# Moving the sums of a feed-forward's seven-product way down from VectorE into accumulating DMAs

## The chip, the cores and the metric

The kernel runs on one core of a Trainium2 chip. Time is device microseconds of one execution; a measurement is the median of several. Engines are named as in the profile: PE is TensorE's matmul, PEld its load of weights, DVE is VectorE, ACT is ScalarE, POOL is GpSimd and SP is SyncE, which here only issues DMAs. A name with a q behind it (SPq, POOLq) is that engine's queue of issued DMAs.

## The reference

One decoder layer in float32 on 1024 tokens of width 1024: a SwiGLU feed-forward, a mixer (stick-breaking attention beside Mamba-2), a cross-attention over 256 memory tokens, and a second feed-forward, each between two RMS norms and with a residual. The change lies in the first feed-forward and in the norms that follow it:

```python
def rmsnorm(x, g):
    x32 = x.astype(jnp.float32)
    y = x32 * lax.rsqrt(jnp.mean(x32 * x32, axis=-1, keepdims=True) + EPS)
    return (y * g.astype(jnp.float32)).astype(x.dtype)

def swiglu(h, w_gu, w_down):
    gu = h @ w_gu
    g, u = jnp.split(gu, 2, axis=-1)
    return (jax.nn.silu(g) * u) @ w_down
...
        f = swiglu(rmsnorm(h, ffn1_pre_g[l]), ffn1_w_gu[l], ffn1_w_down[l])
        h = h + 0.5 * rmsnorm(f, ffn1_post_g[l])
```

The hidden width is 2816, that is 22 blocks of 128.

## The kernel before

Activations lie transposed: 128 features on the partitions, tokens along the free axis, in two halves of 512 tokens (`hh` 0 and 1). Every float32 matmul is made of three with operands split into a high and a low part (`split`, lines 263 and 265: ScalarE copies the high part, VectorE subtracts it for the low one), so a product of one 128 by 128 block costs three matmuls of 512 columns.

The way up (`up_phase`) writes silu(g)·u to HBM, in tiles `act_d[b][hh]` of 128 by 2 by 512; b counts 11 pairs of blocks, and the middle index is the block of the pair. Its last rows in `seven` are VectorE's subtraction at line 818, GpSimd's product at 819 and the store of the second half by GpSimd's queue at 821.

The way down (`down_first`) is one step of Strassen's scheme in Winograd's form: the 2 by 2 split of the work (blocks of a pair, halves of the tokens, halves of the output) takes seven products instead of eight, in the order 1, 5, 2, 6, 3, 7, 4. A product runs over 11 units, one for each pair b; a unit is one activation operand and one weight operand, each split, and 12 matmuls into four PSUM banks. `take` hands the units out and prepares operands five units ahead of PE's program. What runs ahead in fact is bounded by buffers: eight `hl` tiles for split activations, eight places for split weights (`place`), and four raw buffers for what `load` (line 961) brings by SP's queue. Products 5, 6, 3 and 7 take sums of activations: product 5 adds the two blocks of the second half into a buffer `keep[b]` (line 1037), product 6 subtracts a block of the first half from it (1049), product 3 subtracts `keep[b]` from another (1055), and product 7 subtracts two loaded blocks in a raw buffer (1059). All of these go through the helper `add`, so the profile shows them under line 976, by the tiles `xh` (where `keep` lies), `wraw` and `raw`. Weight sums (`wsum`, `wdif`) are made on VectorE in the same way, with a third load for products 1 and 2 (`z`).

After product 2, 6, 3 and so on, the PSUM banks are copied or added into the tiles `F` (`copy`, line 999; `update`, line 1003, again line 976 in the profile). When one half of the tokens is complete, `post` puts its norm into a list of due times on the planner's clock, which adds 0.422 ns for each column of a matmul as PE's program is written: column sums (`rms_cols`, on PE with the column `small`, then lines 332 to 339), row factors (`rms_rows`, lines 347 to 369, with two matmuls), and for each of eight blocks the scaling and residual (lines 428 and 432), a store `h<-F`, the split for the next stage, and `presum`, the squares for the next norm. `sumsq` squares on ScalarE (378, 381) and adds up in two accumulators on VectorE (382); with the eighth block it adds the second accumulator to the first (384). `resid` lists loads of the residual on GpSimd's queue (403). Each engine runs its instructions strictly in the order in which a scheduler at build time put them; that scheduler plays the program through with estimated times, and lets an idle engine take an instruction from far ahead if its buffer is free. `urgent` raises an instruction's priority there.

Of the kernel before, what the change touches and what calls it, by code (L numbers as in the profile page):

```python
# [46 lines left out]
class Kern:  # L47
    def __init__(self, nc, tc, ap):
# [9 lines left out]
        self.kept = {}  # L58

# [314 lines left out]
    def sumsq(self, accs, i, src):  # L374
# [8 lines left out]
        if i == KT - 1:  # L383
            self.kp(nc.vector.tensor_tensor(out=accs[0], in0=accs[0], in1=accs.pop(), op=ALU.add))
# [22 lines left out]
    def post(self, hh, gname, r2, gnext=None, out=None, step=None, spread=True, pins=(23000, 28000), accs=None, tail=None, times=None):  # L407
# [36 lines left out]
        def presum(d):  # L444
            if d == 0:
                accs2.extend(self.new_accs())
            self.sumsq(accs2, d, self.F[hh][d])

        T0 = self.clock
        if step is None:  # L450
# [168 lines left out]
    def up_phase(self, sp, sp2, wgu, gpre, act_d, bank, load, plain, sizes, rw=None, begin=None, between=None):  # L619
# [162 lines left out]
        def seven(f):  # L782
# [34 lines left out]
            with self.urgent():  # L817
                self.emptied = nc.vector.tensor_tensor(out=e, in0=e, in1=b, op=ALU.subtract).ins  # L818
# [19 lines left out]
        def up(f, hh, t, w):  # L838
            ps = self.proj_now(w, hh)
            with self.urgent():  # L840
                nc.vector.tensor_tensor(out=t, in0=t, in1=ps, op=ALU.mult)
# [101 lines left out]
    def seven_tools(self, sp, rw, sums_d=None):  # L943
# [34 lines left out]
        def taker(operands, ahead):  # L978
            order = [(p, b) for p in (1, 5, 2, 6, 3, 7, 4) for b in range(NFF // 2)]
            made, taken = [], [0]  # L980

            def take():
                taken[0] += 1
                while len(made) < min(len(order), taken[0] + ahead):
                    made.append(operands(*order[len(made)]))
# [21 lines left out]
    def down_first(self, sp, rw, wdn, act_d, gpost, gnext):  # L1007
# [13 lines left out]
        def operands(p, b):  # L1021
            a, w = (lambda hh, k: act_d[b][hh][:, k, :]), (lambda k, dh: wdn[b, dh, k])
            tile = place() if p == 1 and b < 2 else self.t(sp, [P, 2, H], F32R, "hl", bufs=8)
            if p == 1:
                x, y = load(a(0, 0), w(0, 0))
                d = wdif[b] = held((self.xp, f"xl{int(b > 3)}", KT + 1))
                nc.sync.dma_start(out=d, in_=w(0, 1))
                o = parts(tile, x), parts(place(), y)
                t = wsum[b] = held(spots[b])
                i = add(t, d, y, ALU.subtract)  # L1030
# [3 lines left out]
            if p == 5:  # L1034
                x, y = load(a(1, 0), a(1, 1))
                k = keep[b] = held((self.xp, f"xh{b // KT}{b % KT}", 1))
                add(k, x, y, ALU.add)
                return parts(tile, k), parts(place(), wsum[b])
            if p == 2:
                x, y = load(a(0, 1), w(1, 0))  # L1040
# [6 lines left out]
            if p == 6:  # L1047
                x, y = load(a(0, 0), w(1, 0))
                add(keep[b], keep[b], x, ALU.subtract)
                o = parts(tile, keep[b]), parts(place(), wsum[b])  # L1050
                add(wsum[b], wsum[b], y, ALU.subtract)
                return o
            if p == 3:
                x, y = load(a(0, 1), w(1, 1))
                add(x, x, keep.pop(b), ALU.subtract)
                return parts(tile, x), parts(place(), y)
            if p == 7:
                x, y = load(a(0, 0), a(1, 0))
                add(x, x, y, ALU.subtract)
# [1363 lines left out]
```

## Time and profile before

| | |
|---|---|
| median of 3 timed runs | 2638.12 us (2637.93 to 2639.47) |
| the profiled execution's own time | 2645.18 us |
| its span, first to last instruction | 2643.4 us |
| mean granted clock of TensorE | 0.992 |
| way down of the first feed-forward (product 1 to the last unit of product 4) | 446.7 to about 673 us of the span |

The profile is of one execution, which took 7.06 us longer than the median of the timed runs; places in it are microseconds from the start of its span. Matmuls overlap: two neighbours start 0.227 us apart at full clock, while one is shown with 0.39 us, so PE's work is best read by counting matmuls in a stretch and looking at the granted clock. An idle engine costs time only where PE waits for it.

### The profile page before, as it was taken

The page shows a single profiled execution, that of the slowest core. Times are in us where ns is not written, and L with a number is a line of the kernel's source. Part 1 is how long each engine was busy: PE and PEld are TensorE (multiplying, and loading weights), DVE is VectorE, ACT ScalarE, POOL GpSimd, SP SyncE. Part 2 cuts the span into 40 slices and gives each one's busy share as a digit, 9 for nine tenths or more (in the row PEclk, how much of TensorE's full clock was granted, in tenths as well). Part 3 has the DMA queues.
Part 4 walks back from the last instruction along what each step waited for, and adds up shares of the span by engine and source line. Part 5 has one row for each costly group of instructions (what it writes and reads, how often), then busy time and mean ns, then how long its engine had stood idle before and what let it go on. Part 6 is the DMA issues. An engine that isn't in the chain of part 4 may idle for free.

```text
span 2643.4 us, 36454 instructions
## 1 busy us (share of the span) xinstructions
PE 2576.9 (97%) x12598; PEld 2135.0 (81%) x12598; DVE 1983.2 (75%) x3085; ACT 1262.9 (48%) x2276; POOL 530.8 (20%) x660
## 2 busy tenths in 40 slices
PE   8999999999999999999999998999999999999998
PEld 6788888887777778888888787887878788888887
DVE  7888787888678774777777777775448989895675
ACT  7544443545367783445554445254445433333432
POOL 1555552001100000000000001122012555542000
PEclk9999999999999999999999999999999999999999
DMA  5688887754721226433434458777667455555976
GB/s 209 238 308 302 304 282 252 255 193 158 259 79 45 71 70 196 115 99 108 109 108 115 146 178 323 252 274 252 218 230 272 167 187 203 195 180 210 347 276 218
DMA packets 225241, 528.87 MB, mean 200 GB/s; under 512 B 28064, under 2 KB 35104, under 8 KB 225056
## 3 DMA queue, kind: packets, MB, share of 16 engines
q1 hardware_dynamic: 190432, 419.56, 48.2%
q0 software_dynamic: 27424, 93.87, 9.8%
q10 hardware_dynamic: 7200, 13.11, 1.3%
q8 instruction: 99, 1.62, 0.3%
q14 instruction: 86, 0.70, 0.1%
HBM read 353.41 MB, written 152.04 MB: 191 GB/s over the span
## 4 chain that ended last, share of the span: by engine, by line
PE 79%; DVE 9%; DMA 6%; ACT 3%; issue 2%; POOL 1%; SPq 0%; DVEq 0%; ACTq 0%; POOLq 0%
PE mm L138 45%; PE dn L138 24%; PE z L138 2%; PE ms L138 2%; PE tr L141 2%; PE y L138 1%; PE ms L141 1%; DMA wraw<-act 1%; DMA raw<-act 1%; DVE hl L265 1%; DVE wlo L265 1%; PE seg L138 1%; DMA blk<-h 1%; DVE whi L265 0%; DMA oraw<-mix 0%
## 5 line engine op out<-in xcount | busy, mean ns | idle before, releaser
L138 PE MATMUL mm<-xh,whi 128*128 128x512 f32 x1288 | 511.5, 406 | 11.1 <-ACT xh L270 7.0
L138 PE MATMUL mm<-xh,wlo 128*128 128x512 f32 x1240 | 478.5, 393 | 3.2 <-DVE wlo L265 2.9
L138 PE MATMUL mm<-xl,whi 128*128 128x512 f32 x1188 | 467.8, 394 | 1.0 <-DVE xl L265 0.7
L138 PEld LDWEIGHTS mm<-xh,whi 128*128 128x128 f32 x1288 | 244.1, 189 | 53.6 <-ACT xh L270 6.9
L138 PEld LDWEIGHTS mm<-xh,wlo 128*128 128x128 f32 x1240 | 234.3, 189 | 55.3 <-DVE wlo L265 3.4
L138 PEld LDWEIGHTS mm<-xl,whi 128*128 128x128 f32 x1188 | 225.6, 190 | 34.1 <-DVE xl L265 1.8
L1823 DVE TENSOR_TENSOR_SCAN nb<-nb,begin 128x128 f32<-128x128 f32 (+7 forms) x128 | 171.7, 1352 | 55.0 <-ACT nb L1819 54.4
L1819 ACT ACTIVATE nb<-z,scale 128x128 f32<-128x128 f32 (+2 forms) x192 | 107.8, 580 | 88.8 <-PE z L138 87.7
L263 ACT CAST whi<-wraw 128x1024 fp32r<-128x1024 f32 (+1 forms) x89 | 81.2, 914 | 69.1 <-PE mm L138 39.1
L1856 POOL MEMSET ath<- 128x128 f32 x64 | 13.1, 205 | 499.0 <-PE mm L138 499.0
L265 DVE TENSOR_TENSOR wlo<-wraw,whi 128x1024 fp32r<-128x1024 f32 x61 | 74.4, 1220 | 38.3 <-ACT whi L263 38.0
L138 PE MATMUL dn<-xh,wlo 128*128 128x512 f32 x296 | 101.0, 389 | 0.0
L737 POOL TENSOR_TENSOR wc<-wraw,raw 128x512 f32<-128x512 f32 x57 | 87.5, 1535 | 66.6 <-DVE whi L265 30.7
L737 POOL TENSOR_TENSOR wc<-raw,wraw 128x512 f32<-128x512 f32 x55 | 85.5, 1555 | 66.5 <-DVE wlo L265 31.4
L819 POOL TENSOR_TENSOR ft<-ft,e 128x512 f32<-128x512 f32 x38 | 62.4, 1642 | 144.2 <-DVE e L818 85.7
L650 ACT ACTIVATE ft<-ft 128x512 f32<-128x512 f32 x88 | 55.4, 631 | 75.0 <-DVE ft L649 70.3
L263 ACT CAST ath<-tr 128x512 fp32r<-128x512 f32 (+1 forms) x107 | 58.2, 545 | 67.5 <-PE tr L141 66.1
L138 PE MATMUL dn<-xh,blk 128*128 128x512 f32 x280 | 90.2, 389 | 0.0
L265 DVE TENSOR_TENSOR atl<-tr,ath 128x512 fp32r<-128x512 f32 (+1 forms) x107 | 67.0, 629 | 29.2 <-ACT ath L263 28.9
L138 PE MATMUL dn<-xh,whi 128*128 128x512 f32 x256 | 88.0, 389 | 0.0
L138 PE MATMUL mm<-ath,v 128*128 128x256 f32 x320 | 86.2, 291 | 0.6 <-DVE sq L1838 0.6
L382 DVE TENSOR_TENSOR acc<-acc,sq 128x512 f32<-128x512 f32 x78 | 52.3, 684 | 42.5 <-ACT sq L381 42.2
(586 smaller groups left out, 6667.9 us busy)
## 6 DMA issues: line engine op xcount, KB each, us to landing
whi<-dwhi SPq DMA_DIRECT2D x57, 512.0 KB, 3.4
wlo<-dwlo SPq DMA_DIRECT2D x57, 512.0 KB, 4.2
wraw<-act SPq DMA_DIRECT2D x102, 256.0 KB, 4.4
raw<-act SPq DMA_DIRECT2D x96, 256.0 KB, 4.3
wraw<-in_w_gu SPq DMA_DIRECT2D x44, 512.0 KB, 4.4
raw<-in_w_gu SPq DMA_DIRECT2D x38, 512.0 KB, 4.8
khi<-whi POOLq DMA_DIRECT2D x30, 512.0 KB, 4.6
klo<-wlo POOLq DMA_DIRECT2D x30, 512.0 KB, 6.7
```

Source lines behind the costliest of these rows:

```text
L138: self._pe(self.nc.tensor.matmul(out, lhsT, rhs, start=start, stop=stop, skip_group_check=self.more), cost)
L141: self._pe(self.nc.tensor.transpose(out, src, self.ident if ident is None else ident), 109.0)
L263: self.kp(self.nc.scalar.copy(hi, src))
L265: (eng or self.nc.vector).tensor_tensor(out=lo, in0=src, in1=hi.bitcast(F32), op=ALU.subtract)
L382: self.kp(nc.vector.tensor_tensor(out=accs[i % 2], in0=accs[i % 2], in1=sq, op=ALU.add))
L650: nc.scalar.activation(t, t, AF.Silu)
L737: nc.gpsimd.tensor_tensor(out=t, in0=a, in1=b, op=op)
L819: nc.gpsimd.tensor_tensor(out=t1, in0=t1, in1=e, op=ALU.mult)
L1819: nc.scalar.activation(nb[:, s0:s1], z[:, 0:n], AF.Sigmoid, scale=sc[:, i : i + 1])
L1823: nc.vector.tensor_tensor_scan(out=nb[:, 0:Wd][:, ::-1], data0=nb[:, 0:Wd][:, ::-1], data1=begin[:, S - Wd : S][:, ::-1], initial=0.0, op0 ...
L1856: nc.gpsimd.memset(x[:, 0, :].bitcast(F32), 0.0)
```

## The change

Sums of activations are no longer made by VectorE. A block is loaded, and the second is added to it by a DMA with `accum_op=ALU.add`, issued on GpSimd's queue. [...] Product 5 loads into `keep[b]` itself and accumulates there; products 6 and 3 accumulate one more block each into `keep[b]`, and load only their weight through a raw buffer; product 7 accumulates in the raw buffer. [...]

The loads get a function of their own, `fetch`, which is called up to three units ahead of `operands`. The third load for product 2 (`z`) stays in `operands`.

In the norms, a flag `apart` makes `sumsq` leave the two accumulators as they are, and `rms_cols`, which already runs over the accumulators of a group, then does its column sums for each. `down_first` sets the flag ahead of the first half's squares and again ahead of the second half's; `post` takes its value over for its own `presum` and clears it, and `presum` sets and clears it around its squares.

```diff
-        if i == KT - 1:
+        if i == KT - 1 and not self.apart:
             self.kp(nc.vector.tensor_tensor(out=accs[0], in0=accs[0], in1=accs.pop(), op=ALU.add))
...
         def presum(d):
             if d == 0:
                 accs2.extend(self.new_accs())
+            self.apart = apart
             self.sumsq(accs2, d, self.F[hh][d])
+            self.apart = False
 
         T0 = self.clock
+        apart, self.apart = self.apart, False
...
-                self.emptied = nc.vector.tensor_tensor(out=e, in0=e, in1=b, op=ALU.subtract).ins
+                x, y = (b, e) if begin else (e, b)
+                self.emptied = nc.vector.tensor_tensor(out=e, in0=x, in1=y, op=ALU.subtract).ins
...
-                nc.vector.tensor_tensor(out=t, in0=t, in1=ps, op=ALU.mult)
+                if begin and hh:
+                    nc.vector.scalar_tensor_tensor(out=t, in0=t, scalar=-1.0, in1=ps, op0=ALU.mult, op1=ALU.mult)
+                else:
+                    nc.vector.tensor_tensor(out=t, in0=t, in1=ps, op=ALU.mult)
...
                 while len(made) < min(len(order), taken[0] + ahead):
+                    if fetch:
+                        while len(got) < min(len(order), len(made) + 3):
+                            got.append(fetch(*order[len(got)]))
+                        made.append(operands(*order[len(made)], got[len(made)]))
+                        continue
                     made.append(operands(*order[len(made)]))
...
+        def plus(x, src):
+            nc.gpsimd.dma_start(out=x, in_=src, accum_op=ALU.add)
+
+        def fetch(p, b):
+            a, w = sources(b)
+            if p == 1:
+                d = wdif[b] = held((self.xp, f"xl{int(b > 3)}", KT + 1))
+                x = load(a(0, 0), w(0, 0))
+                nc.sync.dma_start(out=d, in_=w(0, 1))
+                return x
+            if p == 5:
+                k = keep[b] = held((self.xp, f"xh{b // KT}{b % KT}", 1))
+                nc.sync.dma_start(out=k, in_=a(1, 0))
+                plus(k, a(1, 1))
+                return ()
+            if p == 2:
+                return load(a(0, 1), w(1, 0))
+            if p == 7:
+                x = load(a(0, 0))
+                plus(x[0], a(1, 0))
+                return x
+            if p == 4:
+                return load(a(1, 1))
+            x = load(w(1, int(p == 3)))
+            plus(keep[b], a(0, int(p == 3)))
+            return x
...
             if p == 5:
-                x, y = load(a(1, 0), a(1, 1))
-                k = keep[b] = held((self.xp, f"xh{b // KT}{b % KT}", 1))
-                add(k, x, y, ALU.add)
-                return parts(tile, k), parts(place(), wsum[b])
+                return parts(tile, keep[b]), parts(place(), wsum[b])
...
             if p == 6:
-                x, y = load(a(0, 0), w(1, 0))
-                add(keep[b], keep[b], x, ALU.subtract)
                 o = parts(tile, keep[b]), parts(place(), wsum[b])
-                add(wsum[b], wsum[b], y, ALU.subtract)
+                add(wsum[b], wsum[b], got[0], ALU.subtract)
                 return o
             if p == 3:
-                x, y = load(a(0, 1), w(1, 1))
-                add(x, x, keep.pop(b), ALU.subtract)
-                return parts(tile, x), parts(place(), y)
-            if p == 7:
-                x, y = load(a(0, 0), a(1, 0))
-                add(x, x, y, ALU.subtract)
-                return parts(tile, x), parts(place(), wdif.pop(b))
-            (x,) = load(a(1, 1))
-            return parts(tile, x), parts(place(), wsum.pop(b))
-
-        take = taker(operands, 5)
+                return parts(tile, keep.pop(b)), parts(place(), got[0])
+            return parts(tile, got[0]), parts(place(), (wdif if p == 7 else wsum).pop(b))
+
+        take = taker(operands, 5, fetch)
...
         accs = [self.new_accs(), None]
+        self.apart = True
...
         for i in four:
-            update(F[1][0][i], F[1][0][i], ps[i])
+            update(F[1][0][i], F[1][0][i], ps[i], ALU.subtract)
         for i in four:
-            add(F[1][1][i], F[1][1][i], F[1][0][i], ALU.add)
+            add(F[1][1][i], F[1][0][i], F[1][1][i], ALU.subtract)
...
         units = [take() for _ in range(4)]
+        self.apart = True
         accs[1] = [held((rw, tag, 1)) for tag in ("bh", "bl")]
         squares(1, 1, 0)
         for i in four:
             blocks(ps, units, i, False, True)
-            update(F[1][0][i], F[1][0][i], ps[i], ALU.subtract)
+            update(F[1][0][i], F[1][0][i], ps[i])
             self.sumsq(accs[1], 4 + i, F[1][0][i])
```

More of the change, by code (lines that the diff above doesn't have):

```diff
@@ L446, in presum @@
                 accs2.extend(self.new_accs())
+            self.apart = apart
             self.sumsq(accs2, d, self.F[hh][d])
+            self.apart = False
         T0 = self.clock
+        apart, self.apart = self.apart, False
         if step is None:
@@ L976, in add, with taker @@
             return nc.vector.tensor_tensor(out=o, in0=x, in1=y, op=op)
-        def taker(operands, ahead):
+        def taker(operands, ahead, fetch=None):
             order = [(p, b) for p in (1, 5, 2, 6, 3, 7, 4) for b in range(NFF // 2)]
-            made, taken = [], [0]
+            made, taken, got = [], [0], []
             def take():
@@ L1019, in held, with sources, operands @@
             return self.t(pool, [P, H], F32, tag, bufs=bufs)
-        def operands(p, b):
-            a, w = (lambda hh, k: act_d[b][hh][:, k, :]), (lambda k, dh: wdn[b, dh, k])
+        def sources(b):
+            return (lambda hh, k: act_d[b][hh][:, k, :]), (lambda k, dh: wdn[b, dh, k])
+        def plus(x, src):
[23 more added lines that the diff above has]
+            return x
+        def operands(p, b, got):
+            a, w = sources(b)
             tile = place() if p == 1 and b < 2 else self.t(sp, [P, 2, H], F32R, "hl", bufs=8)
             if p == 1:
-                x, y = load(a(0, 0), w(0, 0))
-                d = wdif[b] = held((self.xp, f"xl{int(b > 3)}", KT + 1))
-                nc.sync.dma_start(out=d, in_=w(0, 1))
+                x, y = got
                 o = parts(tile, x), parts(place(), y)
                 t = wsum[b] = held(spots[b])
-                i = add(t, d, y, ALU.subtract)
+                i = add(t, wdif[b], y, ALU.subtract)
                 if b > 1:
@@ L1034, in operands @@
             if p == 5:
-                x, y = load(a(1, 0), a(1, 1))
-                k = keep[b] = held((self.xp, f"xh{b // KT}{b % KT}", 1))
-                add(k, x, y, ALU.add)
-                return parts(tile, k), parts(place(), wsum[b])
+                return parts(tile, keep[b]), parts(place(), wsum[b])
             if p == 2:
-                x, y = load(a(0, 1), w(1, 0))
+                x, y = got
                 z = self.t(*((self.tp, [P, H], F32, "dg", 1) if b % 2 else (self.fp, [P, H], F32, "rpost", 1)))
```

## The prediction

> **What bounds the kernel now.** I read first the page's busy shares, then the busy time by stretches through the way down (447 to 677 us), and then the timeline wherever a stretch was not full. A stretch's row gives the busy microseconds (and instructions) of PE, PEld, DVE, ACT and POOL behind its length, then the granted clock, the DMA share and GB/s.
>
> ```profile
> span 2643.4 us, 36454 instructions
> ...
> PE 2576.9 (97%) x12598; PEld 2135.0 (81%) x12598; DVE 1983.2 (75%) x3085; ACT 1262.9 (48%) x2276; POOL 530.8 (20%) x660
> ...
> 609.37:614.07 4.70, 0.00 (x1) 0.00 (x0) 4.70 (x9) 3.71 (x7) 0.00 (x0) 0.93 0.17 58
> 614.07:615.94 1.87, 1.87 (x9) 1.87 (x9) 1.87 (x4) 0.00 (x0) 0.00 (x0) 0.50 0.51 149
> 615.94:623.41 7.47, 6.47 (x18) 4.57 (x18) 6.97 (x17) 6.46 (x11) 0.00 (x0) 0.71 0.45 140
> 668.31:677.35 9.04, 8.47 (x27) 6.76 (x27) 6.33 (x14) 2.24 (x4) 1.79 (x4) 0.64 0.88 302
> ```
>
> TensorE sets the time: an edit counts only where it fills a hole on PE. In the changed stage there are two, each followed by a granted clock of 0.50 to 0.71. The timeline (start, duration, engine, line; in brackets the idle time before, and its releaser) shows how the first comes about.
>
> ```profile
> 585.86 1.49 DVE L976 TENSOR_TENSOR wraw<-wraw 128x512 f32<-128x512 f32 x2
> ...
> 593.80 2.88 PE L138 MATMUL dn<-hl,whi 128*128 128x512 f32 x12
> 596.52 2.20 PE L138 MATMUL mm<-hl,wlo 128*128 128x512 f32 x9
> ...
> 601.24 0.69 DVE L976 TENSOR_TENSOR raw<-raw 128x512 f32<-128x512 f32 x1 [2.85 <-DMA raw<-act]
> 606.12 0.69 DVE L976 TENSOR_TENSOR wraw<-wraw 128x512 f32<-128x512 f32 x1 [1.18 <-DMA wraw<-act]
> 606.73 0.68 DVE L265 TENSOR_TENSOR hl<-raw,hl 128x512 fp32r<-128x512 f32 x1
> 607.33 2.47 DVE L976 TENSOR_TENSOR F<-F,dn 128x512 f32<-128x512 f32 x4
> 611.53 1.28 DVE L382 TENSOR_TENSOR acc<-acc,sq 128x512 f32<-128x512 f32 x2
> 613.34 0.68 DVE L384 TENSOR_TENSOR acc<-acc,acc 128x512 f32<-128x512 f32 x1
> 614.07 1.87 PE L138 MATMUL dn<-small,acc 128*128 128x1 f32 x8 [4.70 <-DVE acc L384]
> 618.76 1.28 DVE L265 TENSOR_TENSOR hl<-raw,hl 128x512 fp32r<-128x512 f32 x2
> 620.56 0.15 DVE L332 TENSOR_TENSOR cpost<-dn,cpre 128x4 f32<-128x4 f32 x1
> 622.71 0.50 PE L138 MATMUL dn<-dg,onesr 128*128 128x512 f32 x1 [0.91 <-DVE dg L358]
> ```
>
> A unit of 12 matmuls takes 2.72 us (593.80 to 596.52: 0.227 a matmul); product 3 ends and product 7 begins at 596.5. From then the four updates of F could run, but VectorE does them at 607.3: its queue is in order, and ahead of them stand the adds of product 7 (line 1059), each waiting for two loads. The squares follow late, PE stands 4.70 us at the norm's column sums, and its clock halves. In 609.37 to 623.41, 14.04 us, PE does 18 matmuls (4.08 us at full clock) and 8 records of column sums.
>
> **The change part by part.** The 44 adds of products 5, 6, 3 and 7 leave VectorE.
>
> ```profile
> L976 DVE TENSOR_TENSOR raw<-raw 128x512 f32<-128x512 f32 x5 | 3.4, 687 | 4.6 <-DMA raw<-act 4.6
> L263 ACT CAST hl<-raw 128x512 fp32r<-128x512 f32 x14 | 8.6, 618 | 16.6 <-DVE raw L976 14.1 <-PE ms L138 2.2 <-PE dn L138 0.3
> ...
> wraw<-act SPq DMA_DIRECT2D x48, 256.0 KB, 3.9
> ...
> xl<-in_xT POOLq DMA_DIRECT2D x16, 256.0 KB, 5.7
> h<-F POOLq DMA_DIRECT2D x8, 256.0 KB, 3.0
> ...
> 450.88 2.66 POOL L403 DMA_DIRECT2D xl<-in_xT  x5
> 588.90 0.54 POOL L403 DMA_DIRECT2D xl<-in_xT  x1 [135.36 <-DVE wlo L265]
> ```
>
> (A DMA's row ends with the microseconds from issue to landing.) That is 44 by 0.69, 30 us of VectorE, worth nothing by itself. Their second operands go from SP's queue to POOL's as accumulating DMAs: the bytes fetched stay, POOL gains 44 issues of 0.54 us, 24 us, hidden in a queue that waited 135 us here. Each accumulate waits on POOL for the load whose result it adds to; what can stand behind it are residual loads (line 403) and POOL's last product (line 819), needed tens of microseconds later.
>
> No accumulating DMA is in this trace. Its landing is bounded by the nearest rows on POOL's queue: 3.0 us below (the store), and above twice the load, 11.4, if the destination is read and written again at full price. I take 5.7, the load from HBM into SBUF that it is nearest to. In products 5, 6 and 3 the buffer `keep` is free a whole product (29.9 us) earlier, so even 11.4 is hidden. In product 7 it is not: load, accumulate and split share four raw buffers. One turn of a buffer is T = 3.9 + 5.7 + 1.8 (issue 0.54, splits 0.62 on ScalarE and 0.68 on VectorE) = 11.4 us, with ends 8.7 and 17.1. Four buffers, so a unit in 2.85 us against PE's 2.72, and the operands run up to eight units ahead (buffers of `hl`): no hunger on PE.
>
> The clock of the stall, with estimates from these rows. Product 3 begins at 566.6. Its unit 9 can be split when its unit 1 has freed an `hl`, at 572.0, done at 573.2; its raw buffer then serves units 2, 6 and 10 of product 7, split at 573.2 + T, + 2T and + 3T. The F updates stand behind the split of unit 6 (as at 606.73 before): 596.0, so right at PE's 596.5. From the updates to the last square sum took 5.5 us (607.33 to 612.81): done near 602.5, with 6.9 us in hand before PE's 609.37. The stall goes, and would still go at T up to 15. The next thing late is line 332, which stands behind unit 10's split: 607.4 by the sum. PE comes to the row product 16 matmuls after the column sums, at 614.6, and 332 needs 2.15 us up to it (620.56 to 622.71); so it must start by 612.5, which holds to T = 13.1. With five further splits in the same queue I charge 1 us here (ends 0 and, at T = 17.1, 11.9).
>
> The two parts of the sums: line 384 goes, and PE gets twice the column sums.
>
> ```profile
> 679.62 0.95 PE L138 MATMUL ms<-small,bh 128*128 128x1 f32 x8
> 680.44 0.48 PE L138 MATMUL mm<-xl,whi 128*128 128x512 f32 x1
> ...
> 665.84 0.68 DVE L382 TENSOR_TENSOR acc<-acc,sq 128x512 f32<-128x512 f32 x1
> 667.57 0.68 DVE L384 TENSOR_TENSOR acc<-acc,acc 128x512 f32<-128x512 f32 x1
> 668.31 1.87 PE L138 MATMUL ms<-small,acc 128*128 128x1 f32 x8 [2.54 <-DVE acc L384]
> ```
>
> Eight records take 0.82 us warm (679.62 to 680.44), 1.87 cold. At the first norm nothing waits any more, so this is pure cost: 16 records, 1.64 us. First hole after: 4.08 + 1.64 = 5.72 for 14.04, a gain of 8.3, less the 1 us: 7.3. At the next norm (668) PE waited for line 384; the last part ends at 666.52, 1.7 us before 384 did, so the gain is 1.7 less 0.8 (cold: less 1.9), that is 0.9, with ends of a loss of 0.2 and a gain of 5.7 if the whole hole closed (2.54 + 9.04 us, against 4.3 for its 19 matmuls and 1.64 for the records). By the planner's clock the second half stays in one part: `apart` is one flag, set again after seven units of product 4 (46.7 us from the call of `post(0)`), and the last `presum` of the first half, due at 17.5 + 7 x 4.7 + 0.8 = 51.2, clears it before unit and square number 7 (57). So only two of four norms change.
>
> The signs: three products become the three-operand form.
>
> ```profile
> L841 DVE TENSOR_TENSOR ft<-ft,mm 128x512 f32<-128x512 f32 x3 | 2.1, 684 | 0.6 <-PE mm L138 0.6
> L428 DVE SCALAR_TENSOR_TENSOR F<-F,params,rpost 128x512 f32<-128x512 f32 x16 | 11.9, 743 | 2.1 <-ACT rpost L369 2.1
> ```
>
> 3 by 0.06 us, hidden behind PE; uncovered 0.2. The swapped subtractions keep form and count.
>
> Sum: 7.3 + 0.9 = 8.2 us. Against the profiled execution's own 2645.18 that is 2637.0. The timed median is 2638.12, 7.1 us under that execution; carried over whole it gives 2629.9. If those 7.1 us are partly this stall, the gain is smaller.
>
> The Trainium skill (DMA: Bandwidth & Descriptors, Anatomy of one DMA) puts a DMA from GpSimd at about 2.0 us and its bytes over 436 GB/s, an estimate of 2.6 us for 256 KB. The trace has 5.7 for that load, so the trace decides; by the page T were 7.0, the 1 us would not be charged and the sum 9.2.
>
> **The rivals.**
>
> *The wait goes on to the row product.* For it: VectorE's order, with line 332 behind five more splits. At T between 13.1 and 15.8 (where 332 comes at 620.6, as before) the gain falls from 8.2 to nothing; in the middle 4: time 2634. *The accumulate is slow* (T = 17.1): 332 comes 3.9 us later than now, with 0.8 for the records: 5 us more, 2643.
>
> *Product 1 starves: the other side.* `keep` needs no raw buffer, so nothing but their queues holds product 5's 22 transfers back, and idle queues run ahead: five residual loads asked for in product 3 went out at 450.88.
>
> ```profile
> 446.69 2.66 PE L138 MATMUL dn<-whi,wlo 128*128 128x512 f32 x11
> ...
> 452.38 0.33 SPq L961 DMA_DIRECT2D raw<-act  x1
> ...
> 458.09 0.69 DVE L265 TENSOR_TENSOR hl<-raw,hl 128x512 fp32r<-128x512 f32 x1 [2.72 <-ACT hl L263]
> ...
> 440.00:450.00 10.00, 10.00 (x46) 8.29 (x45) 7.03 (x11) 4.18 (x7) 1.61 (x1) 1.00 0.32 105
> 450.00:460.00 10.00, 10.00 (x45) 8.02 (x44) 6.61 (x11) 2.76 (x5) 3.24 (x6) 1.00 0.81 264
> 460.00:470.00 10.00, 10.00 (x45) 8.28 (x45) 9.13 (x16) 7.21 (x14) 0.00 (x0) 1.00 0.95 325
> ```
>
> Unit 6 of product 1, asked for at 452.38, is split at 458.8 and due at 463.0: 4.2 us in hand, with the DMA full. Units 6 to 10 are 15 transfers, 13 us at 300 GB/s. Shared evenly they take 26, and unit 10 (due 473.9) is ready at 479.7: 6 us lost, net 2 gained, 2636. Wholly behind the 22 (5.8 MB, 19 us) unit 6 is 15 us late: net 7 lost, 2645. It decides from 4.2 us of delay, and costs more than the gain from 12.4. Against it: 440 to 450 runs at 105 GB/s, room for 2 MB. The Trainium skill (the same page, Issuing engines are not separate DMA queues) says all queues share the same 16 engines: by that POOL's queue brings no room.
>
> *It does nothing:* the hole is smaller without the profiler, and the doubled records eat the rest: 2637.
>
> **How the numbers follow.** Forecast (2624 to 2633, by T and the second hole) 0.46; wait at the rows 0.17 (half of it beyond 0.2%); slow accumulate 0.10; product 1 starving 0.19 (a third of it slower); nothing 0.08. 0.2% is 5.3 us, about what a measurement of this kernel can tell: faster below 2632.8, slower above 2643.4. Faster 0.46 + 0.08 = 0.54; slower 0.05 + 0.06 = 0.11; for the operation that no row shows I move 0.04 more to slower, one hundredth of it from faster: 0.53, same 0.32, slower 0.15. Predicted 2629.9, range 2624 to 2643.
>
> **What would show it.** Right: no L976 on `raw<-raw`; F updates near 597; column sums at 609 without idle, 16 records; clock 1.0 at 610 to 620; 16 records at the second norm but 8 on `bh`. Wrong: PE idle between 447 and 477; accumulates landing in over 9 us; line 332 after 613.

## The result, and the profile after

The changed kernel takes 2653.53 us (2651.77 to 2656.07), beside 2638.8 us for the kernel before on the same chip: a ratio of 1.0054, 95% interval 1.0042 to 1.0066. By the ratio it is slower by some 14 us, where 8 us less was forecast and 2643 was the top of the range.

The page says that TensorE did the same work in a longer span (2652.4 us for 2643.4): 16 matmul records more, 46 instructions fewer on VectorE, 44 more on GpSimd.

```profile
PE 2580.9 (97%) x12614; PEld 2138.4 (81%) x12614; DVE 1955.5 (74%) x3039; ACT 1261.8 (48%) x2276; POOL 569.0 (21%) x704
```

The busy time by stretches of the changed kernel shows the place: product 1, where PE had been full (10.00 of 10.00 in both stretches before). The columns are as in the prediction.

```profile
450.00:460.00 10.00, 7.64 (x34) 6.01 (x32) 2.37 (x4) 1.36 (x3) 6.77 (x8) 1.00 1.09 314
460.00:470.00 10.00, 2.85 (x7) 2.23 (x8) 2.87 (x5) 3.52 (x7) 1.25 (x2) 0.62 0.86 185
```

The timeline of the changed kernel tells how it comes about (start, duration, engine, line, operation; in brackets the idle time before and what ended it).

```profile
441.15 2.69 POOL L1038 DMA_DIRECT2D xh<-act  x3 [1.17 <-PE dn L139]
441.20 6.41 SPq L1049 DMA_DIRECT2D xh<-act  x7
446.60 5.60 PE L139 MATMUL dn<-whi,wlo 128*128 128x512 f32 x24
...
451.74 0.87 POOL L1038 DMA_DIRECT2D xh<-act  x1 [7.89 <-DMA xh<-act]
...
456.29 1.76 POOL L824 TENSOR_TENSOR ft<-ft,e 128x512 f32<-128x512 f32 x1
...
458.36 1.13 POOL L826 DMA_DIRECT2D act<-ft  x1
...
466.48 0.62 ACT L264 CAST dx<-wraw 128x512 fp32r<-128x512 f32 x1 [15.11 <-DMA act<-ft]
467.15 8.29 PE L139 MATMUL dn<-hl,dx 128*128 128x512 f32 x24 [9.51 <-ACT dx L264]
```

Read from the end: TensorE waits 9.51 us for the first tile of the tag `dx`. ScalarE, in order, has stood 15.11 us in front of that cast, waiting for the store of the last up-projection block, `act<-ft`: the new tile lies in memory that this store still reads. The store went out at 458.36. It and the product ahead of it (line 824) stand on GpSimd behind accumulates of product 5, each of which waits there for its first load to land; from 443.8 to 451.74 GpSimd does nothing but that. SP's next load for product 1 goes out only at 467.85, the one before it at 454.49. Before, the same chain was there, with nothing ahead of it on GpSimd. The timeline of the kernel before, in rows that the prediction did not use:

```profile
448.39 1.61 POOL L819 TENSOR_TENSOR ft<-ft,e 128x512 f32<-128x512 f32 x1 [16.56 <-issue]
450.30 0.58 POOL L821 DMA_DIRECT2D act<-ft  x1 [0.30 <-POOL ft L819]
...
452.73 0.62 ACT L263 CAST dx<-wraw 128x512 fp32r<-128x512 f32 x1 [3.01 <-DMA act<-ft]
```

The cast waited for that store already, 3.01 us, without costing PE anything. The store is 8.1 us later now (458.36 for 450.30), the cast 13.8 us, and product 7 begins at 608.56 for 596.52: 12.0 us lost. The rest of the cast's delay is the landing of the store itself. The DMA issues from 440 to 480 us show it (a row ends with the microseconds from issue to landing), before:

```profile
act<-ft POOLq DMA_DIRECT2D x1, 256.0 KB, 2.4
```

and in the changed kernel:

```profile
act<-ft POOLq DMA_DIRECT2D x1, 256.0 KB, 8.0
```

So product 5's transfers delay the cast twice: 8.1 us by their accumulates' place in GpSimd's queue, and 5.6 us by a slower landing while the DMA engines are full (share 1.09 in 450 to 460, for 0.81 before).

Downstream, some of the loss comes back. The timeline of the changed kernel at the first norm:

```profile
598.59 0.68 DVE L266 TENSOR_TENSOR hl<-raw,hl 128x512 fp32r<-128x512 f32 x1
...
608.56 2.20 PE L139 MATMUL mm<-hl,wlo 128*128 128x512 f32 x9
...
611.70 0.69 DVE L266 TENSOR_TENSOR hl<-raw,hl 128x512 fp32r<-128x512 f32 x1 [0.66 <-ACT hl L264]
612.31 2.47 DVE L984 TENSOR_TENSOR F<-F,dn 128x512 f32<-128x512 f32 x4
...
621.26 1.84 PE L139 MATMUL dn<-small,acc 128*128 128x1 f32 x16
...
627.13 0.15 DVE L333 TENSOR_TENSOR cpost<-dn,cpre 128x4 f32<-128x4 f32 x1
629.49 0.72 PE L139 MATMUL dn<-dg,onesr 128*128 128x512 f32 x1 [2.63 <-DVE dg L359]
...
688.63 0.95 PE L139 MATMUL ms<-small,bh 128*128 128x1 f32 x8
```

The updates of F start 3.8 us after product 7 (10.8 before), so the column sums come without a wait. The row product waits 2.63 us instead.

For all that follows I use two measures. The ratio is timed. The **way down** is read from a trace: from product 1's first matmul to the first column sum on `bh` (446.60 to 688.63, 242.0 us; before 446.69 to 679.62, 232.9). It leaves out what differs from run to run ahead of it.

### The profile page after: what moved, and what is told of

The parts are those of the page before. It is cut to its first block, busy times and chain, and to the rows that moved or that the text cites. A ratio compares the mean times of both kernels' runs of the same rounds, so it can differ in the third digit from the quotient of the medians.

```text
span 2652.4 us, 36498 instructions
## 1 busy us (share of the span) xinstructions
PE 2580.9 (97%) x12614; PEld 2138.4 (81%) x12614; DVE 1955.5 (74%) x3039; ACT 1261.8 (48%) x2276; POOL 569.0 (21%) x704
## 3 DMA queue, kind: packets, MB, share of 16 engines
q0 software_dynamic: 33760, 105.40, 12.3%
## 4 chain that ended last, share of the span: by engine, by line
PE 85%; DVE 6%; DMA 4%; ACT 2%; issue 2%; POOL 0%; SPq 0%; DVEq 0%; ACTq 0%; POOLq 0%
PE mm L139 47%; PE dn L139 27%; PE ms L139 2%; PE z L139 2%; PE tr L142 2%; PE y L139 1%; PE ms L142 1%; PE seg L139 1%; DMA raw<-act 1%; PE st L139 0%; DVE wlo L266 0%; DMA oraw<-mix 0%; ACT whi L264 0%; DVE F L984 0%; DVE xl L273 0%
## 5 line engine op out<-in xcount | busy, mean ns | idle before, releaser
L1887 POOL MEMSET ath<- 128x128 f32 x64 | 13.1, 205 | 499.0 <-PE mm L139 478.8
```

The costliest lines, as they stand in the source:

```text
L1887: nc.gpsimd.memset(x[:, 0, :].bitcast(F32), 0.0)
```

## The experiments

**How far a trace repeats.** The kernel before, unchanged.

> The kernel before once more, for a second profile beside timed runs. In the first comparison the changed kernel is 14.7 us slower by the timed medians (2653.5 against 2638.8), but only 9.2 us by the two profiled executions (2654.4 against 2645.2): the profiled execution of before was 7 us above its timed median, that of after was not. Theory A: the hole at 609 to 623 us (PE idle 4.7 us at the first norm's column sums, then a halved clock) hangs on the DMAs' luck and is small in most executions. Then this profile, at about 2638 us, shows the idle time before the column sums under 2 us and a clock near 1.0 at 610 to 620. Theory B: profiling itself costs the 7 us; then the profile is again near 2645 us with the 4.7 us in it, while the timed runs stay at 2638.

Measured: ratio 1.0004 (0.9994 to 1.0014). Its second profiled execution, timeline:

```profile
614.60 1.67 PE L138 MATMUL dn<-small,acc 128*128 128x1 f32 x8 [2.19 <-DVE acc L384]
...
680.01 0.95 PE L138 MATMUL ms<-small,bh 128*128 128x1 f32 x8
```

The hole that the prediction set out to fill is 2.19 us here, not 4.70; product 1 began at 449.73, so the way down took 230.3 us. Traces of one kernel differ by 2 to 3 us in this measure, and the hole of the first was on the large side. This execution took 2645.18 us, as long as the first profiled one with twice the hole, so neither theory on record fits: the hole alone is not what puts these two above the median.

**The queue on GpSimd, from two sides.** First, every accumulate is ordered behind the last store:

```diff
-            nc.gpsimd.dma_start(out=act_d[f // 2][1][:, f % 2, :], in_=t1)
+            self.stored = nc.gpsimd.dma_start(out=act_d[f // 2][1][:, f % 2, :], in_=t1).ins
...
-            nc.gpsimd.dma_start(out=x, in_=src, accum_op=ALU.add)
+            i = nc.gpsimd.dma_start(out=x, in_=src, accum_op=ALU.add)
+            self._after(i.ins, self.stored)
```

> The changed kernel, with every accumulating DMA ordered behind the last product and the last store of the way up on GpSimd's queue. In the changed kernel's trace PE waits 9.5 us in product 1 for ScalarE's copy into the first dx tile, which waits for that store: the tile lies where the stored buffer lay. Eight accumulates, each waiting for its load, stand ahead of it on GpSimd's queue. Theory A (the queue's order): with the store first the wait is gone, product 7 begins near 597 us instead of 608.6, and the time falls by 10 to 12 us to about 2642. Theory B (the 22 transfers of product 5 fill the DMA engines and product 1's loads come late): the store leaves early but product 1 still waits for its operands, at least 5 us of PE idle between 447 and 477, and the time stays above 2647.

Second, the last block's product goes to VectorE and its store to ScalarE's queue:

```diff
-            nc.gpsimd.tensor_tensor(out=t1, in0=t1, in1=e, op=ALU.mult)
+            last = begin and f == NFF - 1
+            (nc.vector if last else nc.gpsimd).tensor_tensor(out=t1, in0=t1, in1=e, op=ALU.mult)
...
-            nc.gpsimd.dma_start(out=act_d[f // 2][1][:, f % 2, :], in_=t1)
+            (nc.scalar if last else nc.gpsimd).dma_start(out=act_d[f // 2][1][:, f % 2, :], in_=t1)
```

> The changed kernel, with the last block's product made by VectorE and its second half stored by ScalarE's queue: the accumulates keep their places at the head of GpSimd's queue, but nothing that dx waits for stands behind them. Theory A (the queue's order): as good as ordering the store first, about 2642 us, no wait of dx over 4 us. Theory B (DMA engines full): the transfers start as early as in the changed kernel, so PE still idles 5 us or more in product 1, time above 2647.

Measured: 2646.2 us, 1.0027 (1.0016 to 1.0038), and 2642.17 us, 1.0014 (1.0004 to 1.0023), beside 1.0054 for the change. The waits of TensorE from 446 to 640 us, first kernel (waited for: us in total, times, longest):

```profile
PE dn L139 <- DVE dg L359: 2.2, 1, 2.2
PE dn L139 <- ACT whi L264: 1.5, 2, 0.7
PE dn L139 <- ACT wlo L264: 0.6, 1, 0.6
```

And of the second:

```profile
PE dn L139 <- DVE dg L359: 2.4, 1, 2.4
PE dn L139 <- ACT dx L264: 1.3, 1, 1.3
PE dn L139 <- ACT wlo L264: 0.7, 1, 0.7
```

The wait of 9.5 us is gone in both, and 7 to 11 us of the 14 with it (ratio differences of 0.0027 and 0.0040 at 2640 us). What stays in product 1, 2.1 and 2.0 us of waits, is for splits (ScalarE's casts). In the second kernel, 1.3 us of it is the cast into `dx` once more. Its timeline:

```profile
458.38 0.62 ACT L264 CAST dx<-wraw 128x512 fp32r<-128x512 f32 x1 [6.40 <-DMA act<-ft]
```

The last block's two stores go out at 449.46 and 449.83, and the cast still starts 5.65 us later than the 452.73 of before. The stores land in 6.2 and 8.5 us (2.4 and 2.0 before), and the cast waits for the later one: that is the slow landing alone. An estimate from these rows: the cast can come 4.3 us later at no cost (5.65 less 1.3), so the queue's 8.1 us alone would cost 3.8 us and the slow landing costs 1.3; only the two together make the 9.5. The row product's wait stays too.

**Product 5 without accumulates.** Two loads into raw buffers and one add, as before; the rest as changed.

```diff
-                nc.sync.dma_start(out=k, in_=a(1, 0))
-                plus(k, a(1, 1))
-                return ()
+                return load(a(1, 0), a(1, 1))
...
+                add(k, *got, ALU.add)
```

> Product 5 gets its sums by VectorE adds again (two loads into raw buffers, one add); products 6, 3 and 7 keep their accumulating DMAs, the signs and the norm's two parts stay as changed. The queue theory (the 12 us lost in product 1 come from product 5's early transfers: about 9 from accumulates standing ahead of the last store on GpSimd, about 3 from full DMA engines): the last store is ahead of every accumulate and product 5's loads are held back by the raw buffers, so TensorE waits less than 0.7 us in all of product 1, product 7 starts by 597.5 (596.52 in the profile of before, 608.56 in that of the change), column sums near 610 without a wait, the row product still waits 2 to 3 us; timed 2633 to 2638, ratio 0.9975 to 0.9995. The rival that accumulating DMAs are dear wherever they stand (landing slow, VectorE's splits late in products 6, 3, 7): time stays above 2642 and the waits show in products 6, 3 or 7.

Measured: 2640.32 us, 1.0000 (0.9991 to 1.0009). TensorE's waits from 446 to 640 us, complete:

```profile
PE dn L139 <- DVE dg L359: 3.0, 1, 3.0
```

Product 1 is free of waits, as expected; the time is not as low as expected, since the row product still costs 3 us. Product 5's accumulates cost 0.0054, as much as the whole loss of the change.

**Product 7 without accumulates too, so that only products 6 and 3 have them.**

```diff
             if p == 7:
-                x = load(a(0, 0))
-                plus(x[0], a(1, 0))
-                return x
+                return load(a(0, 0), a(1, 0))
...
+            if p == 7:
+                add(got[0], *got, ALU.add)
```

> Only products 6 and 3 keep accumulating DMAs; products 5 and 7 get their sums by VectorE adds again; signs and the norm's two parts stay as changed. By the queue theory product 1 is free of waits as in the kernel with product 5 alone by adds, and the updates of F stand behind product 7's adds on VectorE again: column sums wait 2 to 4 us (2.2 and 4.7 in the two profiles of before), then the two parts cost 0.8 us: timed 2638 to 2642, ratio 0.9995 to 1.001, some 3 us more than with product 7's accumulates. The rival that product 7's slow accumulates make the row product late (line 333 behind unit 10's split): the row product's wait of 2 to 3 us goes here, and the time is the same or lower than with them, 2635 to 2638.

> The kernel with accumulating DMAs in products 6 and 3 alone, a second time, since its first time (2634.58 us, ratio 0.997) came below what was expected. If the gain is real (the hole from 609 to 623 closed, 615.41 at the row product instead of 623.23): 2632 to 2637, ratio 0.9965 to 0.9985. If it was chance: 2638 to 2642.

Measured: 2634.58 us, 0.9970 (0.9958 to 0.9982), and the second time 2634.91 us, 0.9978 (0.9966 to 0.9990): faster than before, against my expectation that the stall at the column sums would return. The timeline of the first of the two:

```profile
572.82 2.00 SPq L969 DMA_DIRECT2D wraw<-act  x4
...
597.17 0.68 DVE L984 TENSOR_TENSOR wraw<-wraw 128x512 f32<-128x512 f32 x1
597.77 0.69 DVE L266 TENSOR_TENSOR hl<-raw,hl 128x512 fp32r<-128x512 f32 x1
598.37 2.48 DVE L984 TENSOR_TENSOR F<-F,dn 128x512 f32<-128x512 f32 x4
...
609.98 1.84 PE L139 MATMUL dn<-small,acc 128*128 128x1 f32 x16
...
611.86 0.16 DVE L333 TENSOR_TENSOR cpost<-dn,cpre 128x4 f32<-128x4 f32 x1 [0.78 <-PE dn L139]
...
615.41 0.39 PE L139 MATMUL dn<-dg,onesr 128*128 128x512 f32 x1
```

Product 7's adds (line 984) are back ahead of the updates of F, and the updates are early all the same. Its loads go out at 572.82, 126.6 us after product 1's start; before it was 580.45, 133.8 us. So it was not product 7's own adds that made the updates late but how late its loads could begin, and they begin earlier when products 6 and 3 bring only their weights through the raw buffers. Line 333 waits for TensorE now, not TensorE for it. The way down took 225.9 and 223.5 us.

The mirror image is product 7 alone with accumulates: product 5 by adds as above, and products 6 and 3 by

```diff
-            x = load(w(1, int(p == 3)))
-            plus(keep[b], a(0, int(p == 3)))
-            return x
+            return load(w(1, int(p == 3)), a(0, int(p == 3)))
...
+            if p in (6, 3):
+                add(keep[b], keep[b], got[1], ALU.add)
```

The second kernel here is the change with only product 7 put back to adds.

> Only product 7 keeps its accumulating DMAs; products 5, 6 and 3 get their sums by VectorE adds (33 adds of 0.69 us more than in the change); signs and the norm's two parts stay. By the queue theory this is as good as the kernel with product 5 alone by adds, since the adds of 5, 6 and 3 lie behind TensorE's work: no wait over 0.7 us in product 1, updates of F near 597 to 600, column sums near 610, timed 2633 to 2638. If VectorE's extra adds matter they delay the updates of F behind product 7's early operands, and the column sums wait 1 to 3 us: 2637 to 2640.

> The change with product 7 alone put back to VectorE adds; products 5, 6 and 3 keep their accumulating DMAs. Theory: product 5's transfers cost product 1 about 12 us whatever product 7 does, and product 7's accumulating DMAs cost about 3 us at the row product by themselves. So product 1 waits 9 to 10 us for dx as in the change, product 7 starts near 608.5, the row product waits less than 1 us: 2648 to 2652, 2 to 5 us under the change. If the accumulates of product 7 were also what slowed product 1: below 2645.

Measured: 2646.31 us, 1.0023 (1.0013 to 1.0034), against expectation, and 2646.68 us, 1.0020 (1.0009 to 1.0031). The timeline of the kernel with product 7's alone:

```profile
621.98 0.80 PE L139 MATMUL dn<-dg,onesr 128*128 128x512 f32 x1 [6.63 <-DVE dg L359]
```

In the kernel with products 5, 6 and 3 TensorE waits only once from 446 to 640 us: 9.5 us for `dx`.

The two costs are apart: product 7's accumulates make the row product wait (6.63 us alone, 2.2 to 3.0 with those of 6 and 3), product 5's make product 1 wait. Product 7's cost 6 to 9 us as timed (1.0000 against 0.9970 and 0.9978; 1.0054 against 1.0020).

**Which of products 6 and 3.** Product 3's accumulates alone, none at all (with the loads still asked for three units ahead, the other new thing in these kernels), and product 6's alone; all three with the sums of squares in one part. The edit is the last one, for product 6, for both, and for product 3. As in the change, all three store the second half's activations negative, so that sums of activations are additions.

> Accumulating DMAs in product 3 alone; products 5, 6 and 7 by VectorE adds; sums of squares in one part; second half negative. If the gain comes from the raw buffers that product 3's activations no longer take just ahead of product 7: as good as with products 6 and 3, updates of F near 599, no wait at the column sums, 168 to 169 us from product 1's start to the row product, 2634 to 2637. If product 6's accumulates are needed too: updates of F between 600 and 606, part of the wait back, 2637 to 2640.

> No accumulating DMA at all: all sums by VectorE adds, with the loads asked for three units ahead as in the change; sums of squares in one part, second half negative. If the gain of products 6 and 3 comes from their accumulating DMAs: product 7's first loads go out 132 to 134 us after product 1's start as before (133.8; 126 to 127 with the accumulates), updates of F 158 to 161 us after it, the column sums wait 2 to 5 us; timed 2639 to 2642. If the earlier loads alone bring it: 2634 to 2637.

> Accumulating DMAs in product 6 alone; products 5, 3 and 7 by VectorE adds; sums of squares in one part. If product 6's accumulates carry the gain: product 7's loads about 127 us after product 1's start, updates of F near 152, 2634 to 2637. If it takes both, so that each alone moves product 7's loads by 2 to 4 us only: updates of F between 154 and 158, part of the wait at the column sums stays, 2637 to 2640.

Measured: 0.9997 (0.9986 to 1.0009), 0.9994 (0.9986 to 1.0003) and 1.0007 (0.9996 to 1.0018): none differs from before. Product 7's first loads go out at 578.82, 578.72 and 579.58, 131.5 to 132.1 us after product 1's start (133.8 and 132.2 in the two traces of before), and the updates of F come 156.9 to 158.4 us after it (160.6 and 158.1 before, 152.1 and 150.8 with both). So neither product alone, nor the earlier loads alone, moves these dates by much more than two traces of one kernel differ; both products together move the loads by 5.6 to 8.5 us. That raw buffers are what is freed fits this, but the runs show only the dates, not the buffer that decides.

**The two parts of the sums of squares.** Alone on the kernel before; taken away from the change; and taken away from the kernel with products 6 and 3. For the first, the change's lines on the flag were put into the kernel before; for the others it is never set:

```diff
-        self.apart = True
+        self.apart = False
```

> The kernel before with nothing changed but the norm's sums of squares left in two parts (the closing add left out, twice the column sums). Column sums: the wait is 0.7 us shorter, 8 more records cost 0.8 us; second norm: 1.7 us less of wait against 0.8. Timed within 1.5 us of before, ratio 0.9994 to 1.0006. The rival that the two parts are what makes the change slow: 2642 or more.

> The changed kernel, with the flag for two parts never set, so that all sums of squares are joined on VectorE as before. Theory A (each doubled set of column sums costs PE 0.8 us, and the second norm's earlier start gives 1.7 back): within 2 us of the changed kernel's 2653.5. Theory B (the doubled sums make up a good part of the loss): 3 us or more below it.

> Accumulating DMAs in products 6 and 3 alone, and the norm's sums of squares closed to one part as in the kernel before. Against the same kernel with two parts: 0.8 us less at the first column sums (8 records instead of 16), 0.9 us more at the second norm by the prediction's own sum: equal within 1 us, 2633 to 2637. The rival that the two parts are needed to close the hole (the column sums wait for the closing add): 2 us or more slower, with the wait at the column sums.

Measured: 2642.36 us, 1.0004 (0.9995 to 1.0013); 2648.59 us, 1.0032 (1.0018 to 1.0046); 2635.09 us, 0.9976 (0.9964 to 0.9987). TensorE's waits of the first, on either side of the two norms:

```profile
PE dn L139 <- DVE dg L359: 2.2, 1, 2.2
...
PE ms L139 <- DVE acc L383: 0.7, 1, 0.7
...
PE dn L139 <- DVE acc L383: 0.2, 1, 0.2
```

At the second norm the wait for the column sums is 0.7 us for 2.54, as the sum had it. Part of what is gained goes on to the row products: the first norm's waits 2.2 us (0.9 and 0.6 before), the second norm's 0.3 us here and 1.5 us in the first kernel with products 6 and 3 (none before). In time the two parts make no difference, alone or in the fastest kernel. In the change itself the timed difference is 5.8 us (1.0054 to 1.0032; the two intervals overlap a little), of which the trace has 1.8 in the way down (240.2 for 242.0); the 9.2 us in product 1 and 3.25 at the row product stay. Where the rest lies I don't know.

**What is left of product 5's cost.** With the last store off GpSimd and product 7 by adds, so that only product 5's transfers are in question (both edits as above):

> The last block's product and store off GpSimd (as in the second kernel of the first set, 2642.17 us), and product 7 by VectorE adds; products 5, 6 and 3 keep their accumulating DMAs. Theory: 2 to 3 us of waits stay in product 1 from product 5's transfers (full DMA engines), nothing at the column sums, and the row product's wait of 2.4 us goes: 2637 to 2640, so 2 to 4 us above the kernel with accumulates in 6 and 3 alone. If full DMA engines do not matter: level with that kernel, 2633 to 2636.

Measured: 2637.33 us, 0.9987 (0.9977 to 0.9998). TensorE's waits from 446 to 640 us:

```profile
PE dn L139 <- ACT dx L264: 1.1, 1, 1.1
PE dn L139 <- ACT whi L264: 0.7, 1, 0.7
```

It beats the kernel before, and the row product's wait is gone. The 1.1 us for `dx` are again the landing of the last block's stores, 8.0 us for the later one. 2.4 us stay above the kernel with products 6 and 3 (0.9987 to 0.9978), which the two intervals do not separate. Then the first loads of product 5 were put later on SP's queue, by an order behind the last load of the third kind in product 1 (lines 1045 and 1049 of the change):

```diff
-                nc.sync.dma_start(out=d, in_=w(0, 1))
+                self.loaded = nc.sync.dma_start(out=d, in_=w(0, 1)).ins
...
-                nc.sync.dma_start(out=k, in_=a(1, 0))
+                self._after(nc.sync.dma_start(out=k, in_=a(1, 0)).ins, self.loaded)
```

> The kernel with the last block's product and store off GpSimd and product 7 by VectorE adds, and besides product 5's first loads ordered behind product 1's last load on SP's queue (the accumulates follow their loads). If product 5's transfers take the DMA engines from product 1's: TensorE's waits for splits in product 1 (1.1 and 0.7 us there) go, product 1's start to the row product takes 168 to 169.5 us instead of 171.5, timed 2634 to 2636. If it is something else: 171 us and 2637 to 2638 as there. The delay might also make product 5's own operands late: then waits in 477 to 507.

Measured: 2640.34 us, 1.0000 (0.9991 to 1.0009). The edit did the reverse of what I meant. Timeline of its SP queue:

```profile
442.18 7.45 SPq L1050 DMA_DIRECT2D xh<-act  x11
```

All 11 went out in one block ahead of product 1's next load at 452.52 (7 did so in the kernel without the order). The wait for `dx` grew from 1.1 to 2.7 us: more early transfers, more delay. Ordered behind product 1's own activation and weight loads, six units further on:

```diff
-                nc.sync.dma_start(out=k, in_=a(1, 0))
+                self._after(nc.sync.dma_start(out=k, in_=a(1, 0)).ins, ones[min(b + 6, 10)])
```

(`ones` keeps the last such load of each unit of product 1.)

> The last block's product and store off GpSimd, product 7 by VectorE adds, and each of product 5's first loads ordered on SP's queue behind product 1's activation and weight loads of six units further on (the last ones behind unit 10's). If product 5's early transfers take the DMA engines from product 1: no wait of TensorE for splits in product 1, units 6 to 10 asked for by about 461 as in the kernel with accumulates in 6 and 3 alone (468 to 477 with the early transfers), product 1's start to the row product 168 to 169.5 us, timed 2634 to 2636. If not: 171 to 172 us, 2637 to 2638. Product 5's own first operands may come late (load, accumulate and split are about 14 us, from 461): then a wait of up to 3 us appears at 476 instead.

Measured: 2638.16 us, 1.0000 (0.9991 to 1.0009). Timeline:

```profile
458.42 6.52 SPq L1051 DMA_DIRECT2D xh<-act  x11
...
499.96 0.69 DVE L985 TENSOR_TENSOR xh<-rpost,xh 128x512 f32<-128x512 f32 x1 [2.85 <-DMA rpost<-in_w_dn]
...
508.74 3.20 PE L139 MATMUL dn<-hl,whi 128*128 128x512 f32 x11 [1.85 <-DVE hl L266]
```

Its DMA queues from 440 to 510 us (q0 is GpSimd's, with the accumulates alone in it; q1 is SP's; packets, MB, and the share of the 16 engines' time), and its DMA issues (median us to landing at the end):

```profile
q0 software_dynamic: 3168, 5.77, 45.2%
q1 hardware_dynamic: 5616, 10.23, 43.4%
...
xh<-act POOLq DMA_DIRECT2D x22, 256.0 KB, 12.9
xh<-act SPq DMA_DIRECT2D x11, 256.0 KB, 5.8
```

And its stretches at product 1 and product 5:

```profile
447.00:477.00 30.00, 30.00 (x134) 24.84 (x133) 21.53 (x35) 13.39 (x23) 9.61 (x11) 1.00 0.87 265
477.00:507.00 30.00, 29.88 (x132) 24.27 (x130) 15.77 (x25) 14.53 (x27) 9.90 (x12) 1.00 1.11 242
```

Half of the expectation holds: product 1 is full, with its last load out at 457.56. But the time is no better. The accumulates now land in 12.9 us among full DMA engines (share 1.11), product 2's weights (`rpost`) come late, VectorE waits for them, and TensorE waits at the start of product 2. The delay moved; in neither order did product 5's accumulates find a free place between 446 and 510 us. Before, the stretch 477 to 507 moved more, 266 GB/s, at a share of 0.81.

| accumulates in products | beside that | ratio | way down, us |
|---|---|---|---|
| 5, 6, 3, 7 (the change) | | 1.0054 | 242.0 |
| 5, 6, 3, 7 | store first | 1.0027 | 235.5 |
| 5, 6, 3, 7 | last block off GpSimd | 1.0014 | 230.0 |
| 5, 6, 3, 7 | one part | 1.0032 | 240.2 |
| 5, 6, 3 | | 1.0020 | 237.2 |
| 5, 6, 3 | last block off GpSimd | 0.9987 | 227.4 |
| 5, 6, 3 | that, first loads in one block | 1.0000 | 230.2 |
| 5, 6, 3 | that, first loads behind product 1's | 1.0000 | 229.2 |
| 6, 3, 7 | | 1.0000 | 230.3 |
| 7 | | 1.0023 | 234.8 |
| 6, 3 | two runs | 0.9970, 0.9978 | 225.9, 223.5 |
| 6, 3 | one part | 0.9976 | 226.1 |
| 3 | one part | 0.9997 | 231.1 |
| 6 | one part | 1.0007 | 230.6 |
| none | loads three units ahead, one part | 0.9994 | 229.7 |
| none | the kernel before in two parts | 1.0004 | 231.6 |
| none (before) | two traces | 1, 1.0004 | 232.9, 230.3 |

The way down's differences from its mean before (231.6) agree with the timed ones to 5.3 us or better. So most of the change's loss (10.4 of some 14 us) and the gain of products 6 and 3 (5.7 and 8.1 us) lie in the way down. A difference of a few microseconds is below what one trace tells: the kernel with the last block off GpSimd is timed 3.7 us slower than before, and its trace is 1.6 us shorter. The best kernel keeps the accumulates of products 6 and 3 alone and is faster than both kernels of this case: the two-part form by 0.2 to 0.3%, the one-part form by 0.24%.

## Why the prediction was wrong

*The step that failed* is "Each accumulate waits on POOL for the load whose result it adds to; what can stand behind it are residual loads (line 403) and POOL's last product (line 819), needed tens of microseconds later." The product and the store behind it were needed at once: the kernel before has the cast of the first `dx` tile at 452.73, ended by the landing of that very store. I priced the store's delay by who reads its data (product 5) and not by who waits for its source memory to come free. Two orders of the queue take the 9.5 us away, and 7 to 11 us of time. The queue made 8.1 of the cast's 13.8 us; the rest is the store's landing, 8.0 us for 2.4, for which the sum had no term.

*The rival "Product 1 starves"* had the place, the sign and the source (product 5's transfers, with no raw buffer to hold them), at a chance of 0.19. Its mechanism, shared DMA engines, is real: it makes the store's landing slow, and it leaves 2.0 us of waits in product 1 once the queue is mended. But it had the delay come through product 1's loads, and most of it came through a store. It also priced an accumulate's bytes like a load's; the run that ordered product 5's loads behind product 1's shows 45.2% of the engines' time for 5.77 MB of accumulates and 43.4% for 10.23 MB of loads, 1.85 times as much per MB. "440 to 450 runs at 105 GB/s, room for 2 MB" did not help: in the change that stretch is full (259 GB/s at a share of 1.01), and product 5's first loads landed in 9.7 us (median of the 11, 428 to 478). The rule weighed in the prediction, that all queues share the same 16 engines (the Trainium skill, DMA: Bandwidth & Descriptors, Issuing engines are not separate DMA queues), agrees with the run in which the accumulates, moved behind product 1's loads, delayed product 2's.

*Filling the first hole.* The size was right and the cause of it half wrong. The row product comes 169.2 and 167.9 us after product 1's start in the kernel with products 6 and 3, for 176.0 and 173.5 before: 4 to 8 us, where the sum had 7.3. In its clock, the part in which product 3 and the buffers of `hl` set when product 7's units can be split was sound (the load of product 7's unit 2 goes out between 585.3 and 586.8 in the change, 573.3 to 574.8 without the 12.0 us lost earlier, for 573.2 in the sum); that the adds of product 7 had to go as well was not. The sentence "ahead of them stand the adds of product 7 (line 1059), each waiting for two loads" described a symptom.

*The turn of a raw buffer in product 7*, T, was taken as 11.4 us. In the change its splits of units 2, 6 and 10 stand at 598.59, 611.70 and 623.99: turns of 13.1 and 12.3 us, and in the kernel without product 5's accumulates 12.9 and 14.9. Line 333 moreover stands behind a split of product 4's first unit, one turn step further than I put it. So the rival "the wait goes on to the row product" came true as well, from about the T that it named (13.1): 2.63 us, where 1 us was charged. With adds the same turn is 11.4 us (597.77 to 609.19).

The landing was between its bounds. DMA issues of the changed kernel, 428 to 690 us:

```profile
xh<-act POOLq DMA_DIRECT2D x33, 256.0 KB, 6.2
...
raw<-act POOLq DMA_DIRECT2D x6, 256.0 KB, 7.4
wraw<-act POOLq DMA_DIRECT2D x5, 256.0 KB, 5.0
```

5.0 to 7.4 us for 5.7 taken; the issue took 0.87 us on GpSimd where 0.54 was taken. The estimate of 2.6 us by the Trainium skill (DMA: Bandwidth & Descriptors, Anatomy of one DMA) is below all of them.

*The two parts* were priced about right: 16 records in 1.84 us (1.64 taken), 0.7 us of wait left for the second norm's column sums, with up to 1.5 us more at its row product that the sum did not have, the one flag leaving the second half in one part (8 records on `bh` at 688.63), and no difference in time when tried alone.

*The base.* Carrying the whole 7.1 us between the profiled execution and the median over to the result assumed that the hole was as large without the profiler. A second trace of the kernel before had 2.19 us of the 4.70 in the same 2645.18 us; with all of it gone, the best kernel gained 6 to 8 us, so this mattered less than product 5.

## What to carry to other kernels

Before putting work that waits on an engine's in-order queue, list what the scheduler may place behind it, and for each store there ask who is waiting for its source buffer, not only who reads its data; a row in which something already waits for that store without cost is the warning. Ask too what the new transfers do to that store's landing: here it was 5.6 of 13.8 us. Try a replacement product by product: of the four here two together gained 0.2 to 0.3%, and the other two lost 0.5% and 0.2 to 0.3%. A chain of load, accumulate and split in a ring of few buffers is longer than two loads side by side and an add, even where the add costs a busy engine 0.69 us.

## What the runs showed of the hardware that I had not expected

The accumulating DMA's landing follows the load on the engines strongly: 256 KB took 5.0 to 7.4 us in the changed kernel and 12.9 us where they were full, while the plain loads of the same stretch took 5.8 us. In that stretch the DMA share was 1.11 at 242 GB/s, where the kernel before has 0.81 at 266 GB/s. The queue rows of 440 to 510 us put a price on it: 7.8% of the engines' time for each MB of accumulates, 4.2% for each MB of SP's loads. In the same window of the kernel before, GpSimd's plain transfers cost 4.5% (1.57 MB in 7.0%), so it is the accumulating and not the queue that costs 1.75 to 1.85 times as much. And product 3's and product 6's accumulates gained nothing alone (0.9997 and 1.0007) but 0.22 to 0.30% together.
